# A long convolution over even tokens, odd tokens and their sums, in a hybrid decoder block on one core

## The chip, the cores and the metric

The kernel runs on one core of a Trainium2 chip. Its time is the device time of one execution in microseconds (us). Three executions of the kernel before were timed, and their median is the number that the change is held against; one further execution was profiled. The engines are TensorE (PE, matrix products; PEld is its loading of weights), VectorE (DVE), ScalarE (ACT), GpSimd (POOL) and SyncE (SP). In this kernel POOL does little but issue the transfers that add into their target, and SP issues the plain loads and stores.

## The reference, cut to what matters

One layer on 512 tokens of 1024 channels in fp32: a mixer of three branches, then a gated feed-forward part. The change is in branch B, a gated convolution of 31 taps along the tokens, each channel by itself, with a layer norm and a product behind it.

```python
h = rmsnorm(x, norm_mix_g); proj = h @ w_in     # splits into p_a, p_b, q, p_g
...
u, ug = jnp.split(p_b, 2, axis=-1)
u = u * jax.nn.sigmoid(ug)
u = _causal_dwconv(u, conv_b_w) + conv_b_bias   # y_t = sum_k w[k] u_{t-30+k}
u = jax.nn.silu(_layernorm(u, ln_b_g, ln_b_b))
y_b = u @ w_b_out
...
merged = g[:, :, 0] * y_a + g[:, :, 1] * y_b + g[:, :, 2] * y_c   # g: sigmoid gates
x = x + merged @ w_o
...
x = x + (jax.nn.silu(gt) * up) @ w_down         # gt, up: conv3(rmsnorm(x) @ w_up)
out = rmsnorm(x, norm_final_g)
```

## The kernel before

**Products.** Every large product is cut into two by two blocks and done with seven block products instead of eight (forms 1 to 7 of a "quad", `quad_loads`, `multiply`). Each operand is split into a high part (ScalarE rounds it, job `wh` for weights, L1220) and a low part (VectorE subtracts, job `wl`, L1224), and three products hi x hi, hi x lo, lo x hi are added up in PSUM. Some sums of weight blocks are made by a transfer that adds into its target, issued by POOL (`more`, L1374; `wadd` for w_o); others by VectorE.

**Layout and order.** Channels lie on the 128 partitions and tokens along a row; a tile holds two channel groups of 512 tokens. The channels of branch B make four pieces p = 0 to 3. There is no loop that sets the order: every step is a job with a key, an engine and its needs (`Jobs.add`), and the long list `PLAN` gives the order in which jobs are put into the program, the buffer that each new tile takes (sb0 to sb16, lf0 to lf5, wf0 to wf5, the PSUM banks ps0 to ps7), and sometimes one more job that it is held behind. `issue_in_program_order` makes each engine and each queue follow that order strictly, so an instruction that waits holds all behind it on its engine.

**Branch B.** For piece p, ScalarE makes the sigmoid (`sg`), VectorE multiplies (`um`) to give the tile u. The convolution then fills the tile acc:

- `("tap", p, 0)`, ScalarE, L2112: acc = u times the last weight, plus the bias, for each of the two channel groups.
- Taps s = 4, 8, .. 28, VectorE, L2129: one fused multiply-add into acc[s:] from u[:512-s] for each channel group.
- The other 23 taps of each piece (`ACT_TAPS`): ScalarE scales u into a tile of its own (`("tp", p, s)`, L2137), and VectorE adds the tile to acc (`("tap", p, s)`, L2149), one instruction for both groups.
- For the 18 taps in `PAIRED` (five in each of the first three pieces, three in the last) the products of taps s and s + 1 are joined first by a transfer that POOL issues (`("tj", p, s+1)`, L2143: it adds the second tile into the first), and VectorE adds both at once.

When all four pieces are done their sum over channels is made (`tot1`, `tot2`, `mu`), TensorE turns it into the mean (`("mu", "mean")`), and centring, squares, variance, `lns` and `swish` follow. The result is the input of the quads `("out", 1, i)`, with the first 256 tokens (`lo_t`) and the last 256 (`hi_t`) as the two token blocks.

**Merge.** `out_reads` weighs the blocks of `("out", 1, i)` with the gates: `by2` and `by3` treat the first and the second block of tokens of the gate tile m = 2i, `by4` and `by7` the same of m = 2i + 1. `("sum", 1, m, r)` (L2419) adds token half r of gate tile m to what the other branches gave. `mgh` and `mgl` split the merged rows into high and low parts (L2522, L2527); the steps `("ms", p)` make block differences (L2505, L1177); and the products with w_o follow in the order a, b, f, c, d, e, g, each in parts i = 0 and 1 (L1171 to L1173). Products a and b use token half 0. Before the change `("sum", 1, m, 0)` needs only `by2` (or `by4`) and `("sum", 1, m, 1)` only `by3` (or `by7`). The sum of weight blocks `("wsum", i)` (L1640) that c uses is made by VectorE.

**End.** The last products are `("pd", "g", "rest", i)` for the left and right 256 columns (i = 0, 1) of half of the last rows. ScalarE squares and sums each (`("sr", 3, i)`, L3086), `ends` adds the first sum into the second's companion (L3101), a root (L3104), a reciprocal, the scaling and the stores follow.

Of the kernel before, what the change touches and what calls it, by code (L numbers as in the profile page):

```python
# [8 lines left out]
F32 = mybir.dt.float32  # L9
# [5 lines left out]
P = 128  # L15
D = 1024
KC = D // P
SEQ = 512
# [48 lines left out]
ACT_TAPS = [s for s in range(1, 31) if s % 4]  # L67
PAIRED = [(p, s) for p in range(4) for s in (1, 5, 9, 17, 25) if p < 3 or s not in (5, 25)]
# [13 lines left out]
    (("mem tile", 0), "sb2"), (("ldm", 0, 0), ""), (("raw tile", "K"), "wf3"),  # L82
# [883 lines left out]
]  # L966


# [2280 lines left out]
```

## Time and profile before

| | |
|---|---|
| median of three executions | 888.43 us (888.05, 888.43, 890.31) |
| the profiled execution, its own time | 888.78 us |
| its span, first to last instruction | 886.8 us |
| granted TensorE clock | 0.999 |
| PE busy | 878.7 us, 6937 products |
| DVE busy | 827.2 us, 949 instructions |
| ACT busy | 701.4 us, 983 instructions |
| POOL busy | 168.3 us, 193 instructions |
| moved by DMA | 211.38 MB, mean 238 GB/s |

A row of a group reads: line, engine, operation, output <- inputs, shapes, count | busy us, mean ns of one | idle time of the engine just before, and what ended it. A row of the timeline reads: start us, us, engine, line, operation, names, shapes, count, then in brackets the idle time before it and who ended it. A row of the waits reads: who waited <- for whom: us in total, times, longest. A row of the stages reads: the stretch, its length, then busy us (and instructions) of PE, PEld, DVE, ACT and POOL, the granted clock, the share of the DMA engines and GB/s. The chain that ended last follows the work back from the last instruction and gives each engine's share of the span.

### The profile page before, as it was taken

Reading aid. Unit: us, or ns where it says so; the run is one execution under the profiler, and the core shown is the slowest. Engines: PE = TensorE matmul, PEld = TensorE weight load, DVE = VectorE, ACT = ScalarE, POOL = GpSimd, SP = SyncE. Lnnn points to the kernel's source line nnn. Section 1 sums busy time; section 2 is a strip of 40 time slices with the busy share of each in tenths; the row PEclk is TensorE's granted clock in tenths of the full one; section 3 lists DMA queues with packets and bytes.
Section 4 is the critical chain, followed back from the end, with each engine's and each line's share of the span. In section 5 each row is a group of like instructions: output and inputs, shape, how many; then the busy total and the mean of one; then the engine's idle time right before and its main releaser. Section 6 shows DMA issues by size and latency. Waiting matters only on the chain.

```text
span 886.8 us, 17492 instructions
## 1 busy us (share of the span) xinstructions
PE 878.7 (99%) x6937; PEld 848.8 (96%) x6937; DVE 827.2 (93%) x949; ACT 701.4 (79%) x983; POOL 168.3 (19%) x193
## 2 busy tenths in 40 slices
PE   9999999999999999999999999999999999999997
PEld 8999999999999999999899998899999999998886
DVE  6997889989999999999899999998899799999997
ACT  7587889979998788798889973877776677866665
POOL 0012222111222131221221211121121111101120
PEclk9999999999999999999999999999999999999999
DMA  9989999779999999998999999999999799689984
GB/s 352 340 194 234 228 254 233 143 148 211 248 232 265 235 266 218 240 245 223 245 228 257 238 251 283 300 261 244 240 236 260 177 262 190 160 284 331 268 180 131
DMA packets 62288, 211.38 MB, mean 238 GB/s; under 512 B 6784, under 2 KB 11776, under 8 KB 62208
## 3 DMA queue, kind: packets, MB, share of 16 engines
q0 software_dynamic: 28944, 96.00, 59.1%
q1 hardware_dynamic: 32976, 114.02, 35.6%
q8 instruction: 54, 0.88, 0.4%
q10 hardware_dynamic: 288, 0.27, 0.1%
q14 instruction: 26, 0.21, 0.1%
HBM read 194.23 MB, written 4.19 MB: 224 GB/s over the span
## 4 chain that ended last, share of the span: by engine, by line
PE 85%; DVE 6%; DMA 3%; ACT 3%; issue 2%; SPq 0%; POOL 0%; DVEq 0%; ACTq 0%
PE bank L1424 61%; PE bank L1173 6%; PE bank L1171 6%; PE bank L1172 6%; PE bank L1810 2%; DVE wlo L1224 2%; PE bank L2331 1%; PE bank L2333 1%; PE bank L2332 1%; DMA wf<-in_w_in 1%; DMA tp<-tp 1%; ACT whi L1220 1%; DVE fl L1338 1%; DMA wf<-in_w_v 1%; ACT tp L2137 1%
## 5 line engine op out<-in xcount | busy, mean ns | idle before, releaser
L1224 DVE TENSOR_TENSOR wlo<-wf,whi 128x1024 fp32r<-128x1024 f32 (+1 forms) x189 | 226.0, 1209 | 13.5 <-ACT whi L1220 13.1
L1220 ACT CAST whi<-wf 128x1024 fp32r<-128x1024 f32 x192 | 198.1, 1042 | 42.6 <-PE bank L1424 13.0
L2137 ACT ACTIVATE tp<-u,pk 128x495 f32<-128x495 f32 (+22 forms) x184 | 119.2, 712 | 4.7 <-DVE acc L2149 1.9
L2149 DVE TENSOR_TENSOR acc<-acc,tp 128x966 f32<-128x966 f32 (+17 forms) x74 | 87.7, 1185 | 4.0 <-DMA tp<-tp 2.1
L1374 POOL DMA_DIRECT2D wf<-in_w_in x48 | 45.9, 990 | 137.1 <-DVE wlo L1224 63.3
L1424 PE MATMUL bank<-fb10h,whi 128*128 128x256 f32 x232 | 64.1, 276 | 0.3 <-ACT bank L1458 0.3
L1424 PE MATMUL bank<-ft4h,whi 128*128 128x256 f32 x232 | 64.0, 276 | 0.0
L1424 PE MATMUL bank<-fb11h,wlo 128*128 128x256 f32 x232 | 63.9, 275 | 0.0
L1424 PE MATMUL bank<-ft7h,whi 128*128 128x256 f32 x232 | 63.9, 275 | 0.0
L1424 PE MATMUL bank<-fb11h,whi 128*128 128x256 f32 x232 | 63.9, 275 | 0.0
L1424 PE MATMUL bank<-fb00h,whi 128*128 128x256 f32 x232 | 63.9, 275 | 0.0
L1424 PE MATMUL bank<-fb00l,whi 128*128 128x256 f32 x232 | 63.8, 275 | 0.0
L1424 PE MATMUL bank<-fb00h,wlo 128*128 128x256 f32 x232 | 63.8, 275 | 0.0
L1424 PE MATMUL bank<-fb10l,whi 128*128 128x256 f32 x232 | 63.8, 275 | 0.0
L1424 PE MATMUL bank<-fb10h,wlo 128*128 128x256 f32 x232 | 63.8, 275 | 0.0
L1424 PE MATMUL bank<-ft5l,whi 128*128 128x256 f32 x232 | 63.8, 275 | 0.0
L1424 PE MATMUL bank<-ft5h,wlo 128*128 128x256 f32 x232 | 63.8, 275 | 0.0
L1424 PE MATMUL bank<-ft6l,whi 128*128 128x256 f32 x232 | 63.8, 275 | 0.0
L1424 PE MATMUL bank<-ft6h,wlo 128*128 128x256 f32 x232 | 63.8, 275 | 0.0
L1424 PE MATMUL bank<-ft7l,whi 128*128 128x256 f32 x232 | 63.8, 275 | 0.0
L1424 PE MATMUL bank<-ft7h,wlo 128*128 128x256 f32 x232 | 63.8, 275 | 0.0
L1424 PE MATMUL bank<-ft4l,whi 128*128 128x256 f32 x232 | 63.8, 275 | 0.0
(434 smaller groups left out, 3371.3 us busy)
## 6 DMA issues: line engine op xcount, KB each, us to landing
wf<-in_w_in POOLq DMA_DIRECT2D x48, 512.0 KB, 7.9
wf<-in_w_in SPq DMA_DIRECT2D x45, 512.0 KB, 6.4
wf<-in_w_up SPq DMA_DIRECT2D x29, 512.0 KB, 6.2
wf<-in_w_up POOLq DMA_DIRECT2D x26, 512.0 KB, 8.2
wf<-in_w_down SPq DMA_DIRECT2D x15, 512.0 KB, 5.3
wf<-in_w_a_out SPq DMA_DIRECT2D x8, 512.0 KB, 5.6
wf<-in_w_v SPq DMA_DIRECT2D x7, 512.0 KB, 6.1
wf<-in_w_kv SPq DMA_DIRECT2D x7, 512.0 KB, 6.8
```

The costliest lines, as they stand in the source:

```text
L1171: nc.tensor.matmul(ps, s_hi, w_hi, start=start, stop=False, skip_group_check=again)
L1172: nc.tensor.matmul(ps, s_hi, w_lo, start=False, stop=False, skip_group_check=again)
L1173: nc.tensor.matmul(ps, s_lo, w_hi, start=False, stop=stop, skip_group_check=again)
L1220: nc.scalar.copy(parts[0], src())
L1224: nc.vector.tensor_tensor(lo, src(), hi.bitcast(F32), op=ALU.subtract)
L1338: nc.vector.tensor_tensor(t, x, y.bitcast(F32), op=ALU.subtract)
L1374: nc.gpsimd.dma_start(out=tiles[key], in_=block(w, col[c], k), accum_op=ALU.add)
L1424: nc.tensor.matmul(ps[:, c, :], w[:, i, at], in_turns(a[i]), start=first and n == 0, stop=i == 3 and n == 2, skip_group_check=again,)
L1810: nc.tensor.matmul(ps[:, j, :], w[:, k, at], in_turns(a[:, k, :]), start=first and j == 0 and k == 0 and n == 0, stop=g == 1 and k == 3 an ...
L2137: nc.scalar.activation(two(("tp", p, s))[:, j, s:], two(("u", p))[:, j, : SEQ - s], AF.Copy, scale=weight(j),)
L2149: nc.vector.tensor_tensor(a, a, two(("tp", p, at))[:, :, at:], op=ALU.add)
L2331: nc.tensor.matmul(ps, w_hi[:, i, at], hi, start=first, stop=False)
```

## The change

Split the tokens of u into even ones e and odd ones o, and the 31 weights, counted by their delay s, into even delays a (16) and odd delays b (15). The even outputs are a\*e plus b\*o delayed by one; the odd outputs are (a+b)\*(e+o) - a\*e - b\*o. So three filters of 16, 15 and 16 taps over 256 tokens are run per channel group. The tile acc holds a\*e in its first half (r = 0) and b\*o in its second (r = 1); the new tile `cs` holds (a+b)\*(e+o) and e+o. For each k from 1 to 15:

- `("tp", p, k)`, ScalarE: for both groups and both r, u's tokens r, r + 2, .. times the weight of delay 2k + r, 256 - k elements each (k = 15 has r = 0 alone), into one tile;
- `("tap", p, k)`, VectorE: adds that tile to acc; for the ten (p, k) in the new `PAIRED` (k = 1, 7, 13 for three pieces, k = 1 for the last) the tiles of k and k + 1 are joined first by a transfer;
- `("tc", p, k)`, VectorE: two multiply-adds from e+o into the third filter.

New beside them: `("cse", p)` (e+o, VectorE), a start on ScalarE of six instructions (256 elements each), `ole`, `ev` and `od` on VectorE, which put the three filters together, and once `w_sum` (a+b) and `bias_2`. The finished acc holds the even tokens first and then the odd ones, and stays so through the layer norm and the quads of branch B; `out_reads` therefore applies the gates to tokens 0, 2, 4 .. and 1, 3, 5 .., and a token half of the merged sum needs both blocks. `("wsum", 0)` becomes a transfer on POOL. `PLAN` is written anew: the same steps of TensorE, with neighbours swapped in places, other buffers and other holds.

```diff
-ACT_TAPS = [s for s in range(1, 31) if s % 4]
-PAIRED = [(p, s) for p in range(4) for s in (1, 5, 9, 17, 25) if p < 3 or s not in (5, 25)]
+PAIRED = [(p, k) for p in range(4) for k in (1, 7, 13) if p < 3 or k == 1]
...
 def out_reads(q, gates, sigmoids):
+        first, second = (slice(0, SEQ, 2), slice(1, SEQ, 2)) if q[1] == 1 else (lo_t, hi_t)
         def by_bank(i, b):
-            t = parted(gate[i]()[:, :, lo_t])
+            t = parted(gate[i]()[:, :, first])
         def by_tile(i):
-            t = gate[i]()[:, :, hi_t]
+            t = gate[i]()[:, :, second]
...
+        def u_of(j, r, n, p=p):
+            return two(("u", p))[:, j, :].rearrange("p (n r) -> p r n", r=2)[:, r, :n]
+        def u_summed(p=p, u_of=u_of, both_of=both_of):
+            make(("cs", p))
+            t = tiles["u", p].rearrange("p (j n r) -> p j r n", j=2, r=2)
+            nc.vector.tensor_tensor(both_of(1), t[:, :, 0, :], t[:, :, 1, :], op=ALU.add)
...
+            def tap_product(k=k, p=p, rs=rs, u_of=u_of, w=tap_weight):
+                make(("tp", p, k))
+                t = tiles["tp", p, k].rearrange("p (j r n) -> p j r n", j=2, r=2)
                 for j in range(2):
+                    for r in rs:
+                        nc.scalar.activation(
+                            t[:, j, r, k:], u_of(j, r, HALF - k), AF.Copy, scale=w(2 * k + r, j))
+            def tap_add(at, rs, p=p, acc_of=acc_of):
+                t = tiles["tp", p, at].rearrange("p (j r n) -> p j r n", j=2, r=2)
+                a = acc_of()[:, :, rs.start : rs.stop, at:]
+                nc.vector.tensor_tensor(a, a, t[:, :, rs.start : rs.stop, at:], op=ALU.add)
+            def sum_tap(k=k, both_of=both_of, ws=sum_weight):
+                for j in range(2):
+                    a = both_of(0)[:, j, k:]
+                    nc.vector.scalar_tensor_tensor(
+                        a, both_of(1)[:, j, : HALF - k], ws(k, j), a, op0=ALU.mult, op1=ALU.add)
+        def odd_less_even(both_of=both_of, acc_of=acc_of):
+            nc.vector.tensor_tensor(
+                both_of(0), both_of(0), acc_of()[:, :, 0, :], op=ALU.subtract)
+        def even_done(acc_of=acc_of):
+            a = acc_of()[:, :, 0, 1:]
+            nc.vector.tensor_tensor(a, a, acc_of()[:, :, 1, : HALF - 1], op=ALU.add)
+        def odd_done(both_of=both_of, acc_of=acc_of):
+            a = acc_of()[:, :, 1, :]
+            nc.vector.tensor_tensor(a, both_of(0), a, op=ALU.subtract)
...
-                    by = weighed[r : r + 1] if br in OUT_QUADS else weighed
+                    by = weighed
...
-            [("wadd", "x", i), ("wl", ("wo", "d", i))], use=[("wo", "x", i), ("wo", "y", i)]))
+            [("wadd", "x", i), ("wl", ("wo", "d", i))], use=[("wo", "x", i), ("wo", "y", i)])
+            if i else job(
+            ("wsum", i), "POOL", MORE, lambda: nc.gpsimd.dma_start(
+                out=tiles["wo", "y", i], in_=tiles["wo", "x", i], accum_op=ALU.add),
+            [("wadd", "x", i), ("wl", ("wo", "d", i))], MORE_LATENCY,
+            use=[("wo", "x", i), ("wo", "y", i)]))
```

From the new list, the steps of TensorE, VectorE and ScalarE (and `wsum`) from the end of branch B to w_o's b, and the order of the two last products:

```
(("out",1,0),3)  by7(1) by4(0) wl(out,1,1,3) r3(0)  (("out",1,1),3)  by3(0) sum(1,0,1) sum(1,0,0)
sum(1,1,1)  (("out",1,1),4)  mgh(a,0) r3(1) mgl(a,0) by3(1) sum(1,1,0)  (wo,a,0)  by4(1) mgh(a,1)
mgl(a,1) sum(1,2,1) sum(1,2,0)  (wo,a,1)  wsum(0) sum(1,3,1) mgh(b,0) sum(1,3,0) wh(d,1) ms(f)
wn(d,1) mgl(b,0) mgh(f) ms(c)  (wo,b,0)  mgh(b,1) wl(f,0) wh(f,1) wh(c,0) mgl(b,1) mgl(f)  (wo,b,1)
...
(pd,g,5)  (pd,g,rest,0)  ...  (pd,g,rest,1)          before: rest 1, then rest 0
```

More of the change, by code (lines that the diff above doesn't have):

```diff
@@ L614 @@
-    (("sum", 1, 1, 0), ""), ((("out", 1, 1), 3), ""), (("r3", ("out", 1, 0)), ""),
-    (("mgh", "a", 1), ""), (("wl", ("wo", "a", 1)), ""), (("mgh", "b", 0), "sb3"),
-    (("wl", ("wo", "d", 0)), "", (("out", 1, 0), 3)), (("by3", ("out", 1, 0)), ""),
-    ((("out", 1, 1), 4), ""), (("mgl", "a", 1), ""), (("r3", ("out", 1, 1)), ""),
-    (("sum", 1, 0, 1), "sb12"), (("wadd", "x", 0), "", (("out", 1, 1), 3)),
[105 rows of a table removed]
-    ((("cf", 1, 1), "done"), ""), ((("cf", 1, 0), "done"), ""), (("silu", 1), ""),
[18 rows of a table removed]
-    ((("cf", 2, 1), "done"), ""), ((("cf", 2, 0), "done"), ""), (("silu", 2), ""),
[34 rows of a table removed]
@@ new lines @@
+    (("r2", ("gate", 1, 1)), "sb10"), (("var", "sum"), ""), ((("gate", 1, 1), 6), ""),
+    (("wh", ("merge", 0, 3, 1)), ""), (("r3", ("gate", 1, 0)), ""),
+    (("sum", 0, 2), "", ("r2", ("gate", 1, 1))), (("var", "fold"), ""), (("sigmoid", 1, 0), ""),
[5 rows of a table added]
+    (("table", "swish"), ""), (("wl", (("gate", 1, 1), 4)), ""),
+    (("ld", (("out", 1, 0), "u")), "lf2", ("v", "squares")), (("wh", ("wo", "b", 1)), ""),
+    (("v", "rows"), "ps5"), (("ld", (("out", 1, 1), "s")), "wf2", ("v", "squares")),
+    (("r5", ("gate", 1, 1)), "sb14"), ((("gate", 1, 1), 7), ""), (("lns", 0), ""),
[3 rows of a table added]
@@ new lines @@
+    (("wadd", "x", 1), "", (("out", 1, 0), 4)), (("by3", ("out", 1, 0)), ""),
+    (("sum", 1, 0, 1), "sb13"), (("ld", ("wo", "y", 1)), "lf4", ("r6", ("out", 1, 1))),
+    (("sum", 1, 0, 0), "sb2"), (("sum", 1, 1, 1), ""), ((("out", 1, 1), 4), ""),
[5 rows of a table added]
+    (("wsum", 0), "", ("mgl", "a", 1)), (("sum", 1, 3, 1), ""), (("mgh", "b", 0), "sb8"),
[98 rows of a table added]
+    ((("cf", 1, 0), "done"), ""), ((("cf", 1, 1), "done"), ""), (("silu", 1), ""),
[122 rows of a table added]
+    ((("cf", 8, 0), "done"), ""), ((("cf", 8, 1), "done"), ""), (("silu", 8), ""),
[115 rows of a table added]
@@ L1124, in scaled_act @@
         return n / 1160.0 + 0.175 + extra
-    TAP = 0.665
+    TAP, TAP_HALF = 0.665, 0.4
     MM, MM_HALF, MM_QUAD = 0.2158, 0.114, 0.1119
@@ L2112, in conv_start @@
                 nc.scalar.activation(
-                    two(("acc", p))[:, j, :], two(("u", p))[:, j, :], AF.Identity,
-                    bias=par("conv_b_bias", 2 * p + j),
-                    scale=par("conv_b_w", (K_B - 1) * KC + 2 * p + j),
-                )
-        job(("tap", p, 0), "ACT", 2 * scaled_act(512, 0.09), conv_start,
-            [("um", p), ("ldp",)] + ([("tap", p - 1, K_B - 4)] if p else []),
-            take=[(("acc", p), ANY)], use=[("u", p)])
-        made_taps = []
@@ L2172, in first_sum @@
+        both_use = [("acc", p), ("cs", p)]
+        job(("ole", p), "DVE", dve(512), odd_less_even, [made_taps[-1], ("tc", p, K_B // 2)],
+            use=both_use)
+        job(("ev", p), "DVE", dve(512), even_done, [("ole", p)], use=[("acc", p)])
+        job(("od", p), "DVE", dve(512), odd_done, [("ev", p)], use=both_use)
+    conv_done = [("od", p) for p in range(4)]
     def first_sum(key, a, b):
```

297 lines of the change are left out of this document (143 added, 154 removed), and 1534 rows, old and new, of the table PLAN.

## The prediction

> **What bounds the kernel now.** I read the profile's page first (engine sums, the chain that ended last), then the stages, then who made TensorE wait, and only then the groups the change touches.
>
> ```profile
> span 886.8 us, 17492 instructions
> ...
> PE 878.7 (99%) x6937; PEld 848.8 (96%) x6937; DVE 827.2 (93%) x949; ACT 701.4 (79%) x983; POOL 168.3 (19%) x193
> ...
> PE 85%; DVE 6%; DMA 3%; ACT 3%; issue 2%; SPq 0%; POOL 0%; DVEq 0%; ACTq 0%
> ```
>
> TensorE (PE) is busy 99% of the span and carries 85% of the chain that ended last. VectorE (DVE) at 93% looks nearly as full, but carries 6%. The kernel is bound by TensorE; the question is how much of its 886.8 - 878.7 = 8.1 us of idle time the change can reach.
>
> ```profile
> 1.05 3.78 PE L2734 MATMUL bank<-ones 128*128 128x128 f32 x16 [1.05 <-DVE ones L2737]
> ```
> ```profile
> 881.04 0.28 PE L1173 MATMUL bank<-whi,zl 128*128 128x256 f32 x1
> 881.35 0.38 ACT L3086 ACTIVATE j<-bank 128x256 f32<-128x256 f32 x1 [1.20 <-PE bank L1173]
> 881.63 0.19 ACT L3086 ACTIVATION_READ_ACCUMULATOR j<-bank 128x1 f32 x1
> 881.86 0.16 DVE L3101 SCALAR_TENSOR_TENSOR cols<-cols 128x1 f32<-128x1 f32 x1 [1.67 <-ACT j L3086]
> 882.05 0.29 ACT L3104 ACTIVATE cols<-cols 128x1 f32<-128x1 f32 x1 [0.23 <-DVE cols L3101]
> ```
>
> 1.05 us lie before the first product and 886.8 - 881.32 = 5.5 us behind the last one. So only 8.1 - 1.05 - 5.5 = 1.6 us of idle time stand inside the run. The waits of TensorE name them:
>
> ```profile
> PE bank L2734 <- DVE ones L2737: 1.1, 1, 1.1
> PE bank L1171 <- ACT ob L2032: 0.7, 1, 0.7
> PE bank L1424 <- ACT bank L1458: 0.3, 1, 0.3
> PE bank L1173 <- DVE ql L1944: 0.2, 1, 0.2
> PE bank L1810 <- DVE wlo L1224: 0.2, 1, 0.2
> PE bank L1173 <- DVE mgl L2527: 0.2, 1, 0.2
> ```
>
> The first row is the start; the other five sum to 1.6 us. The stages say the same of the stretch where the long convolution runs:
>
> ```profile
> 200.00:300.00 100.00, 100.00 (x876) 99.36 (x875) 96.66 (x109) 92.08 (x135) 24.48 (x26) 1.00 1.01 237
> 300.00:400.00 100.00, 99.74 (x890) 99.39 (x890) 98.47 (x105) 85.20 (x121) 22.44 (x25) 1.00 1.02 242
> 400.00:500.00 100.00, 100.00 (x716) 94.59 (x716) 93.16 (x101) 88.89 (x122) 18.98 (x21) 1.00 0.98 238
> ```
>
> After the window and its length come PE, its weight loads, DVE, ACT and POOL busy in us. TensorE is idle 0.26 us in 300. VectorE and ScalarE (ACT) run close to full beside it and keep up.
>
> **The change part by part.** *The products.* The new order holds the same 386 groups of TensorE steps, some swapped with a neighbour; no product goes. TensorE: 0.
>
> *The convolution's arithmetic.* Taps 4, 8 .. 28 were multiply-adds on VectorE, the others were scaled by ScalarE and added by VectorE, some after a joining transfer.
>
> ```profile
> L2137 ACT ACTIVATE tp<-u,pk 128x495 f32<-128x495 f32 (+22 forms) x184 | 119.2, 712 | 4.7 <-DVE acc L2149 1.9 <-DVE yal L2259 1.1 <-DMA tp<-tp 0.7
> L2149 DVE TENSOR_TENSOR acc<-acc,tp 128x966 f32<-128x966 f32 (+17 forms) x74 | 87.7, 1185 | 4.0 <-DMA tp<-tp 2.1 <-ACT tp L2137 0.5
> L2129 DVE SCALAR_TENSOR_TENSOR acc<-u,pk,acc 128x508 f32<-128x508 f32 (+6 forms) x56 | 38.5, 728 | 0.1
> L1882 DVE SCALAR_TENSOR_TENSOR hb<-x,pk,rows 128x256 f32<-128x256 f32 x16 | 6.4, 473 | 0.0
> L2112 ACT ACTIVATE acc<-u,pk 128x512 f32<-128x512 f32 x8 | 6.1, 806 | 0.4 <-DVE u L2105 0.4
> L1525 DVE TENSOR_TENSOR g<-g,yy 128x512 f32<-128x512 f32 x8 | 5.5, 684 | 0.0
> ```
> ```profile
> 7.54 0.91 ACT L1591 ACTIVATE mh<-mem,pk 128x256 fp32r<-128x256 f32 x2
> ```
> ```profile
> 540.93 1.21 DVE L1640 TENSOR_TENSOR wo<-wo,wo 128x1024 f32<-128x1024 f32 x1
> ```
>
> VectorE loses 87.7 + 38.5 us, and 1.2 us for the weight sum that becomes a transfer: 127.4. It gains the summed filter, 15 steps x 2 halves x 4 pieces = 120 multiply-adds of under 256 elements, at 6.4/16 = 0.40 us in a row of such: 48.0 (at 473 ns each, were none to overlap, 56.8); 60 - 10 = 50 adds, 46 of about 1000 elements at 1.185 = 54.5 and four of half that at 0.68 = 2.7; 16 steps of 512 (the sum of even and odd tokens, and three to close each piece) at 0.68 = 10.9. Two more steps run once, on the weights and the biases, at most 0.68 each by the same row. Sum 116.1 without them, so VectorE is relieved of some 10 to 11 us (1 to 2.5 at the dear end). ScalarE loses 119.2 + 6.1 = 125.3 and gains 232 scalings and 24 starts of under 256 elements, at 0.91/2 = 0.455: 116.5, so 9 us less. That bound is soft: the trace shows no ScalarE read of every second element in SBUF. If each short step cost what a long one does now (119.2/184 = 0.648), it would be 166, 41 us more. I take 0.455, because reads of every second element are in this trace from PSUM (line 1470 reads its bank so), and they cost nothing:
>
> ```profile
> L1470 DVE TENSOR_TENSOR gt<-gt,bank 128x512 f32<-128x512 f32 x14 | 9.5, 681 | 0.2 <-PE bank L1424 0.2
> ```
>
> 681 ns against 684 ns for line 1525, which reads SBUF in order. [...]
>
> In time all this is worth 0: both engines lie beside TensorE, which is idle 0.26 us in the stretch where the saving falls. The cover that hides the saving is TensorE's own queue.
>
> *The joins.* Eighteen joining transfers become ten. One wait of the present order comes from a join:
>
> ```profile
> 186.26 2.01 ACT L1940 ACTIVATE qh<-qq 128x1024 fp32r<-128x1024 f32 x2 [3.14 <-DMA tp<-tp]
> ```
> ```profile
> 186.26 2.48 DVE L2149 TENSOR_TENSOR acc<-acc,tp 128x1022 f32<-128x1022 f32 x2 [2.11 <-DMA tp<-tp]
> ```
>
> Both engines stand until a join lands, the query parts come late, and TensorE pays twice soon after: 0.7 for ob and 0.2 for ql. In the new order the summed filter's steps, which need no transfer, stand ahead of that add, and the score products are elsewhere. I take -0.9; between 0 (another step late in their place) and -0.9.
>
> *The merge behind branch B.* This is where the change adds a wait. The tokens of branch B now come out as even and odd, so each half row of the merged sum needs two products of gate and branch (by2 and by3, or by4 and by7) where it needed one. The first half rows, which the w_o products a and b use first, now wait for the last products of branch B.
>
> ```profile
> 534.26 0.38 PE L1171 MATMUL bank<-whoh,mgh 128*128 128x512 f32 x1
> ```
> ```profile
> 579.41 2.68 PE bank L1424 x24
> ```
> ```profile
> 868.22 0.38 PE L1172 MATMUL bank<-wlo,zh 128*128 128x512 f32 x1
> 868.43 0.38 PE L1173 MATMUL bank<-whi,zl 128*128 128x512 f32 x1
> ```
> ```profile
> 535.05 0.74 DVE L1518 SCALAR_TENSOR_TENSOR g<-bank,g 128x256 f32<-128x256 f32 x2
> 535.72 0.68 DVE L2419 TENSOR_TENSOR mg<-g,g 128x512 f32<-128x512 f32 x1
> 536.32 0.68 DVE L2527 TENSOR_TENSOR mgl<-mg,mgh 128x512 fp32r<-128x512 f32 x1
> 536.92 1.22 DVE L2505 TENSOR_TENSOR mg<-mg,mg 128x1024 f32<-128x1024 f32 x1
> 538.05 1.22 DVE L1224 TENSOR_TENSOR wlo<-wo,whi 128x1024 fp32r<-128x1024 f32 x1
> ```
>
> Starts tell the pace on VectorE: 0.60 us for 512 elements, 1.13 for 1024, 0.67 for the pair. TensorE takes 2.68 us for 24 products of 256 columns, and 12 x 0.215 = 2.6 for each part of a and b. Let 0 be the start of the product (out,1,1),3; the (out,1,0),3 before it is then done. Nine steps of 512 stand in the new order (r3, by3, three sums, r3, the low part of a's first half, by3, a sum): 0.2 + 5.4 = 5.6, with a's first part needed at 5.4 and ready at 4.5. Then by4 0.67, a's second low part 0.60: 6.9, needed at 8.0. Then four sums 2.4, the difference f 1.13, b's first low part 0.68: 11.1, needed at 10.55, so TensorE stands 0.6. Then the difference c, a weight's low part and b's second low part reach 14.0 against 13.7, another 0.25. Together 0.85 against 0.2 in the same place now (the wait for mgl): +0.6. I bound it by -0.2 (no wait at all) and +2 (VectorE 1.4 us late at time 0, somewhat more than one 1024-element step).
>
> *The weight sum by transfer* is queued on POOL behind a's second low part (at 6.9), ahead of two other weight adds there, and ScalarE has the high part of w_o's c queued behind its landing.
>
> ```profile
> tp<-tp POOLq DMA_DIRECT2D x4, 510.0 KB, 7.1
> ```
>
> It lands near 6.9 + 7.1 = 14, plus 1 for the queue; c begins behind a, b and the four parts of f, near 5.4 + 10.4 + 0.85 + 5.2 = 21.8. High and low part take 2.2 us, so 4 us of cover remain: 0. Landing 4 us later it would be paid one for one.
>
> *The end.* The two last products change places, so the square that comes last writes where the root reads, and the add at 881.86 is done before: the root follows the square directly, 882.05 - 881.82, about -0.2.
>
> **Sum.** The profiled execution took 888.78 (886.8 span and 2.0 around it): 888.78 - 0.9 + 0.6 - 0.2 = 888.3. That execution lies 0.35 above the median of the three runs, 888.43; against the median I predict 887.9.
>
> **Rivals.** *Faster:* every wait inside goes, 1.6, and the end gives 0.2: 886.6. To pass 0.3% (2.7 us, about what a measurement of this kernel tells from none) another 0.9 must come from the start or from products stretched by a late operand that no wait row lists: 885.5. For it: 11 us of relief on VectorE. Against: the windows from 200 and from 400, in which TensorE is never idle, have nothing to give. *Slower, by reads of every second element:* ScalarE 41 us dearer over the stretch of the adds:
>
> ```profile
> L2149 DVE TENSOR_TENSOR acc<-acc,tp x74: 1153/1184/1224, 95.3 to 457.1; 128x1022 f32<-128x1022 f32 x4, 128x1018 f32<-128x1018 f32 x4, 128x1014 f32<-128x1014 f32 x4, 128x1010 f32<-128x1010 f32 x4
> ```
>
> That is 362 us, so 11 in each 100: 92 + 11 = 103 in the window from 200, 3.1 us too many, the next two at 96 and 100, an estimated 1 us more: 892. It decides from about 0.6 us a step. Against it stands the PSUM row. *Slower, by the merge:* VectorE comes late to time 0 above. It has 5.6 us of work for 5.4 of TensorE's there, so what it is late goes on to TensorE one for one, and from 3.2 us of lateness the run is slower by over 0.3%: 891.2 at 3.3. Against it: in the profile of before by4 started at 535.05, only some 0.5 us behind the end of its product (534.26 + 0.28). *The change brings nothing it says:* a second order of the same work has new small waits for the old ones, 888.4; it lies within my forecast.
>
> **How the numbers follow.** My forecast, within 0.3% (885.8 to 891.1), 0.73: nothing on TensorE's path is taken away, and the terms sum to -0.5. Faster 0.14. Slower 0.13: reads 0.05, merge or another stage whose wait grows like it 0.08. The terms' own ends give 888.43 - 0.9 - 0.2 - 0.2 = 887.1 and 888.43 + 2 = 890.4; to hold 8 in 10 the range reaches into both rivals, 885.5 to 891.0.
>
> **What would show it.** In the new profile: PE busy again 878 to 879 us with 6937 products; DVE near 817 and ACT near 692; the 256-element scalings near 0.4 to 0.46 us in a row; ten tp joins and no TensorE wait for ob or ql; a wait for mgl of about 0.6 near 540. I am wrong if TensorE's idle time inside the run passes 4 us or the scalings take 0.6 us.

## The result and the profile after

| | before | after |
|---|---|---|
| median of all runs beside each other | 889.18 us (888.05 to 890.31, 4 runs) | 897.90 us (895.24 to 899.30, 4 runs) |
| profiled execution, its span | 888.78, 886.8 | 897.00, 895.2 |

The changed kernel is slower: the ratio is 1.0099, 95% interval 1.0081 to 1.0118. The forecast was 887.9 (885.5 to 891.0). One execution of one later kernel, e13, ran at a granted clock of 0.753 and is left out; e16 is the same kernel again.

The page of the changed kernel, its first lines and the chain:

```profile
span 895.2 us, 17542 instructions
...
PE 882.3 (99%) x6937; PEld 849.8 (95%) x6937; DVE 820.8 (92%) x1006; ACT 705.1 (79%) x1047; POOL 159.7 (18%) x186
...
PE 30%; DVE 0%; ACT 0%; issue 0%; DVEq 0%
```

VectorE fell by 6.4 us, ScalarE rose by 3.7, TensorE still has 6937 products, and the span grew by 8.4. (The chain is followed for only 30% of the span here, so it can't be set beside the 85% of before.) The waits of TensorE name places (columns: sum in us, times, longest):

```profile
PE bank L2244 <- ACT mu L2218: 1.3, 1, 1.3
PE bank L1151 <- DVE x L2626: 1.1, 1, 1.1
PE bank L2778 <- DVE ones L2781: 1.1, 1, 1.1
PE bank L1404 <- ACT bank L1438: 0.8, 2, 0.6
PE bank L1404 <- DVE wlo L1204: 0.8, 1, 0.8
PE bank L2244 <- DVE mu L2222: 0.6, 1, 0.6
PE bank L1153 <- DVE mgl L2571: 0.5, 1, 0.5
PE bank L1152 <- DVE wlo L1204: 0.5, 1, 0.5
```

The waits for ob and ql of before are gone; new ones stand at the channel mean (mu, L2244), in w_o (L1151 to L1153) and at weight tiles (wlo). Waits leave out products that were only stretched (TensorE is busy 882.3 us for its 6937 products here, 878.7 before), so I use a second reading throughout: **lateness**, the start of the n-th TensorE product in a kernel minus the start of the n-th in the profile of before. Both kernels have the same 6937 products.

| n-th product, its time before | 3200th, 380 us | 3750th, 456 | 3900th, 474 | 4400th, 536 | 4450th, 547 | 4800th, 598 | 5400th, 665 | last, 881 |
|---|---|---|---|---|---|---|---|---|
| after: late by | -1.42 | -0.11 | 2.91 | 2.71 | 3.34 | 5.82 | 8.24 | 8.57 |

So 1.4 us are gained by 380 us; then 4.3 are lost between 380 and 474 us (1.3 before the mean, with one TensorE wait of 0.60 us at 415 us, and 3.0 at the mean), 0.6 at the merge, 2.5 in w_o behind it, 2.4 at the start of the up projection. Behind the last product 0.2 is gained.

The first loss is a loss of VectorE's time. Stretches of 15 us before and behind the last adds, first in the kernel before, then in the changed one (after the window: PE, PEld, DVE, ACT, POOL busy in us):

```profile
440.00:455.00 15.00, 15.00 (x83) 13.46 (x82) 14.47 (x17) 15.00 (x24) 4.07 (x5) 1.00 1.01 204
455.00:470.00 15.00, 15.00 (x123) 14.60 (x122) 14.87 (x16) 11.00 (x15) 2.62 (x3) 1.00 1.04 248
```
```profile
440.00:455.00 15.00, 15.00 (x83) 13.47 (x82) 11.55 (x16) 13.52 (x24) 3.63 (x5) 1.00 0.97 200
455.00:470.00 15.00, 12.78 (x97) 11.72 (x96) 14.88 (x19) 10.83 (x15) 1.76 (x2) 1.00 0.93 196
```

Before, VectorE is idle 0.66 us of the 30; after, 3.57. The difference, 2.9, is as large as the lateness behind the mean; the runs below show what causes it. VectorE stands idle first, while TensorE is still fully busy, and TensorE pays 10 us later. What VectorE waits for, in the changed kernel (ScalarE's and VectorE's timelines, then TensorE's):

```profile
448.27 2.17 ACT L2152 ACTIVATE tp<-u,pk 128x243 f32<-128x243 f32 x4
451.68 2.16 ACT L2152 ACTIVATE tp<-u,pk 128x242 f32<-128x242 f32 x4 [1.24 <-DVE acc L2164]
```
```profile
453.87 1.17 DVE L2164 TENSOR_TENSOR acc<-acc,tp 128x968 f32<-128x968 f32 x1 [1.02 <-ACT tp L2152]
454.95 1.22 DVE L1204 TENSOR_TENSOR wlo<-wf,whi 128x1024 fp32r<-128x1024 f32 x1
456.19 0.66 DVE L2164 TENSOR_TENSOR acc<-acc,tp 128x482 f32<-128x482 f32 x1
456.88 0.69 DVE L2191 TENSOR_TENSOR cs<-cs,acc 128x512 f32<-128x512 f32 x1
```
```profile
464.33 0.51 PE L2244 MATMUL bank<-mu,mean_w 128*128 128x512 f32 x1 [1.35 <-ACT mu L2218]
```

ScalarE makes the products of one delay step in four short instructions, 2.17 us. It then waits 1.24 us for VectorE's add, because the next products go to the same buffer, and VectorE then waits 1.02 us for ScalarE. The two work in turn instead of side by side. Behind the last add (456.19) stand three closing steps, the sum, the fold and the mean's parts.

### The profile page after: what moved, and what is told of

Its sections match the earlier page's. It is cut to its first block, busy times and chain, and to the rows that moved or that the text cites. A ratio compares the mean times of both kernels' runs of the same rounds, so it can differ in the third digit from the quotient of the medians.

```text
span 895.2 us, 17542 instructions
## 1 busy us (share of the span) xinstructions
PE 882.3 (99%) x6937; PEld 849.8 (95%) x6937; DVE 820.8 (92%) x1006; ACT 705.1 (79%) x1047; POOL 159.7 (18%) x186
## 5 line engine op out<-in xcount | busy, mean ns | idle before, releaser
L1204 DVE TENSOR_TENSOR wlo<-wf,whi 128x1024 fp32r<-128x1024 f32 x204 | 244.3, 1212 | 22.7 <-ACT whi L1200 19.5
L1200 ACT CAST whi<-wf 128x1024 fp32r<-128x1024 f32 (+1 forms) x207 | 213.9, 1046 | 38.8 <-PE bank L1404 11.4
L2152 ACT ACTIVATE tp<-u,pk 128x255 f32<-128x255 f32 (+14 forms) x232 | 114.8, 585 | 3.6 <-DVE acc L2164 2.4
L1354 POOL DMA_DIRECT2D wf<-in_w_in x57 | 50.9, 951 | 209.8 <-PE bank L1404 48.4
L1404 PE MATMUL bank<-ft6h,whi 128*128 128x256 f32 x232 | 64.0, 276 | 0.2 <-ACT gt L1434 0.2
L1404 PE MATMUL bank<-ft5h,whi 128*128 128x256 f32 x232 | 63.9, 275 | 0.0
L1404 PE MATMUL bank<-ft4h,wlo 128*128 128x256 f32 x232 | 63.8, 275 | 0.0
```

The source lines that it names most:

```text
L1200: nc.scalar.copy(parts[0], src())
L1204: nc.vector.tensor_tensor(lo, src(), hi.bitcast(F32), op=ALU.subtract)
L1354: nc.gpsimd.dma_start(out=tiles[key], in_=block(w, col[c], k), accum_op=ALU.add)
L1404: nc.tensor.matmul(ps[:, c, :], w[:, i, at], in_turns(a[i]), start=first and n == 0, stop=i == 3 and n == 2, skip_group_check=again,)
L2152: nc.scalar.activation(t[:, j, r, k:], u_of(j, r, HALF - k), AF.Copy, scale=w(2 * k + r, j))
```

## The experiments

All are compared with the kernel before on the same chip. "Lost" is the growth of lateness in the profiled execution. The first four were written for four theories: A, ScalarE's short steps hold back the last piece's adds; B, VectorE's own queue behind the last add (three closing steps and two weight tiles' low parts) makes the mean late; C, the new list's order is worse whatever the steps cost; D, the weight sum's transfer lands late and holds ScalarE, VectorE and TensorE in turn.

| run | median us | ratio to before, 95% | lost 380 to 474 | at 474 late by | lost 547 to 598 | lost 598 to 665 |
|---|---|---|---|---|---|---|
| after | 897.90 | 1.0081 to 1.0118 | 4.3 | 2.9 | 2.5 | 2.4 |
| e10 (kernel before) | 891.98 | 1.0018 to 1.0044 | 2.0 | 2.3 | 1.3 | 0.0 |
| e17 | 893.18 | 1.0031 to 1.0069 | 0.2 | -1.9 | 2.1 | 2.7 |
| e16 | 897.13 | 1.0068 to 1.0106 | 0.7 | 1.5 | -0.3 | 2.4 |
| e13 (as e16, three executions) | 896.15 | 1.0054 to 1.0098 | | | | |
| e18 | 893.69 | 1.0035 to 1.0073 | 0.4 | 0.2 | -0.3 | 2.3 |
| e1 | 895.58 | 1.0052 to 1.0095 | 4.0 | 2.1 | 2.3 | 3.6 |
| e9 | 895.48 | 1.0047 to 1.0090 | 4.2 | 3.3 | 1.9 | 2.3 |
| e3 | 897.63 | 1.0080 to 1.0133 | 5.9 | 4.3 | -0.3 | 2.3 |
| e6 | 898.15 | 1.0085 to 1.0115 | 4.6 | 3.1 | 1.5 | 2.5 |
| e11 | 897.53 | 1.0059 to 1.0116 | 6.0 | 5.6 | 2.3 | 2.8 |
| e14 | 897.96 | 1.0079 to 1.0121 | 4.9 | 3.4 | 2.3 | 2.0 |
| e2 | 896.08 | 1.0058 to 1.0107 | 4.2 | 3.6 | 1.1 | 2.3 |
| e5 | 896.31 | 1.0061 to 1.0107 | 2.4 | 2.0 | 0.8 | 3.8 |
| e7 | 904.66 | 1.0143 to 1.0195 | 6.6 | 6.3 | -0.3 | 0.3 |
| e4 | 896.15 | 1.0048 to 1.0105 | 3.7 | 2.2 | 1.1 | 1.0 |
| e8 | 893.51 | 1.0035 to 1.0065 | 2.9 | 2.6 | 1.1 | 0.0 |
| e12 | 894.85 | 1.0033 to 1.0073 | 4.8 | 4.6 | 0.1 | 0.2 |
| e15 | 895.53 | 1.0045 to 1.0086 | 4.6 | 4.6 | -0.2 | 1.3 |

One warning for this table: after, e2, e4 and e5 are the same program up to 474 us, and stand there at 2.9, 3.6, 2.2 and 2.0 us. e7 is the same program up to the mean, and its first product of the mean comes 3.8 us late, against 1.4, 2.1, 0.7 and 0.5 in those four. Even at 380 us the profiles of the new list stand between 2.0 us early and 0.8 late, and the 1.3 us lost before the mean in the changed kernel are not lost in e5. Single executions differ by that much, so at the mean only e17 and e18, whose medians fell too, say something by themselves.

**Has VectorE time to spare?** e10, on the kernel before:

```
+        for _ in range(3 if key == ("tot",) else 1):
             nc.vector.tensor_tensor(tiles[key], tiles[a], tiles[b], op=ALU.add)
...
+            for _ in range(2 if p == "d" else 1):            # low part of the merged d
+            for _ in range(2 if unit in ((("up", 5), 1), (("up", 5), 2)) else 1):   # wl
```

> On the kernel before, with its own order: VectorE repeats work that it has done anyway, in three places: the first sum of the mean twice more (2.3 us, near 451), the low part of the merged d once more (1.1 us, near 550), and the low parts of two weight tiles of the up projection once more each (2.3 us in all, near 690). If VectorE has no time to spare in the first two stages and TensorE follows it, the lateness grows by about 1.8 to 2.3 us at the mean and by about 1.1 us in the w_o stage, by nothing at 690, and the time is 892 to 892.6. If VectorE's idle 8 per cent cover such things, as the forecast had it, the time stays at 889.2.

VectorE's added work at the mean and the first TensorE wait behind it:

```profile
450.47 3.74 DVE L2176 TENSOR_TENSOR tot<-acc,acc 128x1024 f32<-128x1024 f32 x3
```
```profile
PE bank L2207 <- ACT mu L2181: 0.6, 1, 0.6
```

Lost: 2.0 us at the mean for 2.3 added, 1.3 in w_o for 1.1 added, 0.4 near 670 (where the third addition fell) for 2.3 added. The median is 891.98, 3.2 above the kernel before beside it (888.77). In the first two stages VectorE's added time is nearly all paid by TensorE, although VectorE is busy only 93% of the span; in the third it nearly isn't.

**Why is the mean late?** Three runs that move nothing in the order. e17, ScalarE's time of the last piece:

```
+                if p == 3:
+                    nc.scalar.activation(t[:, :, :n_r, k:], u[:, :, :n_r, : HALF - k],
+                                         AF.Copy, scale=w(2 * k, 0))
+                    return
```

> The changed kernel with one longer step of ScalarE (about 1.1 us) in place of the four (2.1 us) for each delay of the last piece alone; all of that piece's even and odd products and both its channel blocks take one weight, so its result isn't the reference's. VectorE's work is unchanged. If ScalarE's time is what starves VectorE before the mean, the lateness gained there falls from 2.9 to 1 us or less. If VectorE's closing steps or the buffers that the products wait for set it, it stays at 1.5 to 3.

e16 (and e13 before it), VectorE's closing steps of the last piece:

```
         def odd_less_even(both_of=both_of, acc_of=acc_of, p=p):
+            if p == 3:
+                return
...          (the same in odd_done)
```

> On the changed kernel with its own order: two of the three closing steps of the last piece are left out (the subtraction of the even result from the sums and the last subtraction, 0.69 and 0.68 us of VectorE, so that piece's odd results are not what the reference has). If every microsecond of VectorE in front of the mean is paid by TensorE, the lateness gained at the mean falls from 2.9 to 1.5 us and the time by about 1.4, to about 896.5. If the transfer's landing or ScalarE sets the mean, it stays near 2.9.

> The edit of e13 once more, since its profiled execution ran at a granted clock of 0.753 and can't be read by stages: two closing steps of the last piece left out, 1.37 us of VectorE. If VectorE's work in front of the mean is paid one for one, the lateness gained at the mean falls from 2.9 to about 1.5 us; if ScalarE or a landing sets it, it stays near 2.9.

e18 is both edits:

> Both edits of the two runs beside it: one step of ScalarE for each delay of the last piece, and its two closing steps left out. If the two causes add, the mean is no longer late: the lateness gained there is between minus 0.3 and 0.4 us, and the time is 2.5 to 3 us below the changed kernel's, about 895. If something else sets the mean, 1 us or more remains.

e17's loss is gone altogether. Its last adds and the mean, VectorE's timeline of e17:

```profile
449.21 1.17 DVE L2169 TENSOR_TENSOR acc<-acc,tp 128x968 f32<-128x968 f32 x1 [0.45 <-ACT tp L2152]
450.30 1.22 DVE L1204 TENSOR_TENSOR wlo<-wf,whi 128x1024 fp32r<-128x1024 f32 x1
451.43 0.65 DVE L2169 TENSOR_TENSOR acc<-acc,tp 128x482 f32<-128x482 f32 x1
```

The last add starts at 451.43 instead of 456.19, and the mean's first product at 460.92 instead of 464.33, where the same program without the edit spread from 463.4 to 466.7. TensorE does not wait for the mean, and the median falls by 4.7 us (the ratio from 1.0099 to 1.0050). One step of about 1.5 us (1.41 to 1.61) in place of four that take 2.1 was enough: ScalarE's time per delay in the last piece sets the mean. e16 stands at 1.5 us late where the changed kernel stood at 2.9: by 1.4, the 1.37 us that were taken away. But its first product of the mean came only 0.6 earlier (463.75), which is inside the spread, so this one execution does not show that VectorE's closing steps count. Its median did not fall; in the profile the next stage lost 5.1 us, most of it to a transfer (below). e18 has no wait for the mean either, but since e17 alone removes it, e18 can't show whether the two edits add.

e1 shortens ScalarE's time less:

```
-                    for r in rs:
-                        nc.scalar.activation(
-                            t[:, j, r, k:], u_of(j, r, HALF - k), AF.Copy, scale=w(2 * k + r, j))
+                    nc.scalar.activation(
+                        t[:, j, :n_r, k:], u[:, :n_r, : HALF - k], AF.Copy, scale=w(2 * k, j))
```

> The changed kernel, but ScalarE scales even and odd tokens of a tap in one step with the even tap's weight (116 longer steps in place of 232 short ones; the odd delays thus get the wrong weights). It takes away ScalarE's cost per short step and nothing from VectorE or the order. Theory A (short steps on ScalarE hold the last piece's adds back, so the channel mean comes late): the adds wait for no scaling any more, the mean's product starts about 3 us earlier (464.3 to about 461.5), and the run gains 2.5 to 3 us. Theory B (VectorE's own queue behind the last add makes the mean late: three closing steps and two weight lows before it): the last add comes earlier by the waits seen, 1 to 2 us, and the mean by as much at most. Theory C (the order of the whole list is worse, whatever the steps cost): no gain over 0.5 us.

The median fell by 2.3, a little less than A wanted; the mean's product started at 463.49, not near 461.5, and the place at 474 (2.1 instead of 2.9) lies inside the warning. Its steps were dearer than planned, 0.85 us each instead of 0.65 (last section), so it took little of ScalarE's time away, and e17 is the better test.

The rest of these runs try to mend the order in front of the mean by moving entries of the list or giving a tile another buffer. e9 (the job is also allowed to take a `wf` buffer):

```
-    (('tp', 3, 13), 'sb3'),
+    (('tp', 3, 13), 'wf1'),
```

> One edit on the changed kernel: the products of delay step 13 of the last piece go to a buffer of the weights' ring, so ScalarE no longer waits for VectorE's add of step 13 before it writes step 14 (1.24 us of wait in the changed kernel; both steps shared one buffer). If VectorE's idle time in front of the last adds is what the mean pays, the mean product starts about 1.2 us earlier, the lateness gained there falls from 2.9 to about 1.8 us, and the time to about 896.7. If VectorE's queue behind the last add is the limit, neither moves.

The wait of 1.24 us was gone and the mean's share of the loss fell from 3.0 to 2.1 us, as expected in size; the median fell by 2.4, but the stretch as a whole lost as much as before. By the warning above this stays undecided. e3 and e6 shorten VectorE's queue behind the last add (`wl` of form 4 behind `("mu", "low")`; in e6 also `tot2` right behind `tot1`):

> The changed kernel, with one entry moved: VectorE's low part of the weight of (gate,1,0),4 goes from before the closing step od of the last piece to behind the low part of the mean's sums. Theory B: the mean comes 1.1 us earlier (one 1024-element step) and the run gains about 1.1 us. Theory A: 0 to 0.3 us, since ScalarE's lateness is ahead of it.

> Two edits on the changed kernel: the weight low part for form 4 of gate (1,0) moves behind the mean's low part on VectorE (as before), and the transfer that adds the third pair's result into the sum moves to right behind the first add in GpSimd's order, ahead of a weight add that was held. If it was this transfer's landing (461.4 us) that kept the mean late once VectorE's queue was shortened, the mean product starts at 462.8 to 463.4 instead of 464.3 and the time falls by 1.0 to 1.5, to about 896.5. If the last adds themselves are late (short ScalarE steps), the mean stays within 0.4 us of where it was, and so does the time.

Neither helped. In e3 the sum then waited 0.90 us for the transfer `tot2`. In e6 it did not, and the mean's product started at 463.39, as was expected for the transfer; but the same program as the changed kernel reached 463.4 too (e5). In both runs form 4 waited 1.4 us for VectorE right behind the mean: here the work that was put off was missed a little later. e11 (e9, and `("sigmoid", 0, 2)` and one weight tile's two parts behind the last products) and e14 (e9, and the tile for which ScalarE waits at 420 us behind step 7):

> On the changed kernel, three local edits in front of the mean: the second buffer as in the run beside it; one sigmoid (two steps, 1.3 us) moved behind the last full products; and one weight tile's high and low part moved behind the last products and the last add. ScalarE then reaches the last products about 2.5 to 3.7 us earlier. If ScalarE's steps and waits starve VectorE there, the lateness gained at the mean falls from 2.9 to between 0 and 1 us and the time to about 895.3. If not, it stays at 1.8 or more and the time at 896.7.

> Two local edits on the changed kernel: the second buffer for step 13, and one weight tile's high part and scaled part (for the merge of branch A) moved behind the products of step 7 on ScalarE. In the changed kernel ScalarE waited 3.9 us for that tile's load at 420 to 424 us with step 7 queued behind it, and VectorE stood idle 2.4 us. If such waits of ScalarE are where VectorE's time before the mean went, step 7 starts 4 to 5 us earlier, and the lateness gained between 400 and 470 us falls from 4.2 to 1 to 2 us; the time is 894 to 895.5. If VectorE's work alone sets it, it stays at 3.3 or more, as with the second buffer alone.

Both failed. In e11 VectorE waited 1.18 us for the last products, since the tile that used to fill that time was now behind them. In e14 step 7 waited 3.57 us for its buffer in place of the load, and the tile that I had moved came 2.9 us late for its own product. None of the moves that were tried brought the mean back.

**w_o.** The path of the weight sum in the changed kernel, over POOL, ScalarE, VectorE and TensorE:

```profile
539.36 0.86 POOL L2525 DMA_DIRECT2D wo<-wo  x1 [1.98 <-DVE mgl L2571]
```
```profile
549.72 1.06 ACT L1200 CAST whi<-wo 128x1024 fp32r<-128x1024 f32 x1 [4.43 <-DMA wo<-wo]
550.68 1.03 ACT L2566 CAST mgh<-mg 128x1024 fp32r<-128x1024 f32 x1
```
```profile
551.75 1.23 DVE L2571 TENSOR_TENSOR mgl<-mg,mgh 128x1024 fp32r<-128x1024 f32 x1 [2.26 <-ACT mgh L2566]
```
```profile
554.86 0.45 PE L1151 MATMUL bank<-whi,mgh 128*128 128x512 f32 x1 [1.11 <-DVE x L2626]
```

The transfer lands 10.3 us behind its issue. ScalarE holds the merged high part c behind it, VectorE stands idle 2.26 us, and TensorE's lateness grows by 2.5 us up to 559 us, with waits of 1.11 us (554.86) and 0.49 (558.77). e2 moves `("wh", ("wo", "c", 0))` behind `("mgh", "d")`; e5 gives the sum back to VectorE, behind `("ms", "c")`:

> The changed kernel, with one entry of the list moved: ScalarE's high part of w_o's c, which waits for the weight sum by transfer, goes behind the high parts of the merged rows c and d instead of ahead of them. Theory D (the transfer lands late and holds what is queued behind it on ScalarE, from there VectorE's low part and row adds, from there TensorE): the waits at 553 to 559 us, 2.5 us in sum, go or fall to 0.5, and the run gains about 2 us. Rival (the wait is in the merge's new dependency, not in the transfer): they stay.

> One edit on the changed kernel: the weight sum for c of half 0 is done by VectorE again (1.2 us, behind the merged difference c) instead of by a transfer from GpSimd's queue. If the transfer's landing is what is late (10.3 us from issue to the end of ScalarE's wait in the changed kernel), the waits of TensorE at 553 to 559 us go, the lateness gained in the w_o stage falls from 3.1 to about 1 us, and the time to about 895.5. If instead VectorE's own queue is the limit there, the sum's 1.2 us pushes the row adds and c's low part back by as much, and the time stays at 897 to 899.

In e2 the loss fell from 2.5 to 1.1. In e5 it fell to 0.8, but the part before it (536 to 547 us) rose from 0.6 to 1.8, where b's low part now came behind the sum: together 2.6 against 3.1. So VectorE's 1.2 us cost about as much as the transfer did. e12 (below) issues the transfer without the hold and puts c's high part behind the function table's load (1.28 us), and loses 0.1, though the landing took 12.2 us there. With e2 that points to the transfer's place, and not to the transfer itself.

A second transfer comes in from e16, its tile whol (low part of b's weights):

```profile
L1221 POOL DMA_DIRECT2D whol<-in_w_o x3: 859/859/862, 527.5 to 543.4; - x3
...
  PE bank L1152: 3.6, 1
...
DMA to landing us min/median/max: 8.4/8.5/8.9
```

POOL issues b's at 535.99 here and at 536.52 in the changed kernel; before, at 524.00. In the changed kernel it lands 5.4 us later, and the product that uses it starts at 542.37: 0.4 us to spare. In e16 it lands 8.9 us later, and TensorE waits 3.6. What moved it is the new list's place for the load of these weights, which SP issues at 492.32 before, at 525.61 in the changed kernel and at 524.51 in e16; ScalarE rounds and scales the tile behind that, and in e16 it waits for the load itself:

```profile
533.17 1.05 ACT L1200 CAST whoh<-wf 128x1024 fp32r<-128x1024 f32 x1 [0.90 <-DMA wf<-in_w_o]
```

In the changed kernel the scaling also stands behind a's high part, which waits 1.82 us for the merged sum. So the change took this transfer's cover away. The same wait, 2.5 to 3.3 us, is in the profiles of e3, e4 and e18. How much of the spread among executions comes from it was not measured.

**The order of the list.** e4 takes before's order of all jobs from behind w_o's c; e7 takes before's order, merge and weight sum from the mean on:

> The changed kernel up to the last step of w_o's c, and from there the order of the list of before (its buffers too, where they are free). No arithmetic differs from the changed kernel. Theory C for the third stretch of lost time (2.4 us at 607 to 624 us, in the up projection, which the convolution's change does not touch): the waits there go, and the run gains about 2.4 us. Rival (the lateness is handed down from the stages before): they stay, whatever the order.

> The changed kernel up to the channel mean, then the kernel before: its order of all work from the mean on, its merged sums over the two contiguous halves of the tokens (so branch B's tokens are added in another order than the output wants), each of which needs only its own half of the branch, and the weight sum on VectorE. If merge, transfer and order behind the mean are what costs the later 5.5 us, the lateness stays flat from 470 us on (within 0.7) and the time is 891.5 to 892.5. If the later losses are only what the late mean leads to, they stay and the time is 896 to 898.

In e4 the stretch from 598 to 665 us lost 1.0 us instead of 2.4, and the median fell by 1.8. In that stretch every profile with the new list loses 2.0 to 3.8 us, those with the old order 0.0 to 1.3 (e4, e7, e8, e12, e15). There the new list has the loads for the first weight tiles of the up projection in another order. In the changed kernel ScalarE waits for one, and behind it TensorE:

```profile
606.46 1.05 ACT L1200 CAST whi<-wf 128x1024 fp32r<-128x1024 f32 x1 [2.21 <-DMA wf<-in_w_up]
```
```profile
608.82 0.38 PE L1404 MATMUL bank<-fb11h,wlo 128*128 128x256 f32 x1 [0.77 <-DVE wlo L1204]
```

Which load's place is at fault was not tried by itself. e7 otherwise failed as an experiment: it was already 3.8 us late at the mean's first product, where it is still the changed kernel's program, and TensorE later waited 4.2 us for one merged low part alone. I take it that the old order expects VectorE's work to be further on there than it was; that was not tried by itself.

**All together.** e8 is the w_o edit of e2, e6 and e4's order; e12 and e15 have e4's order and the earlier transfer, with e11's and e14's mean stage:

> Four local edits together, with the computation of the changed kernel: form 4's weight low part behind the mean, the sum's transfer earlier, the high part of w_o c behind the merged high part d, and the list of before from behind w_o c. If the parts' gains add (1.0 to 1.5 at the mean, 1.3 in w_o, 1.4 in the up projection), the time is about 894; if they stand in for one another, 895.5 to 896.5. In neither case does it beat the kernel before (889.3).

> All repairs together, with the computation of the changed kernel: the mean stage of the run beside it; in w_o the weight sum's transfer without its hold on a merged low part, and c's high part behind the function table's load, where ScalarE stands idle; and the list of before from behind w_o c. If the parts add (1.4 us gained before the mean, 0.5 lost there, 0.6 at the merge, 0.3 in w_o, none behind it, 0.2 gained at the end), the time is 889 to 890.5, the same as before. If an unlisted cost of the changed convolution remains, it stays above 892.

> The repairs of the run beside it, the sum's transfer earlier, the w_o edits (the weight sum's transfer without its hold, c's high part behind the table load) and the list of before from behind w_o c, all with the computation of the changed kernel. If they add: 1.4 us gained before 380 us, 1 to 2 lost before the mean, 0.6 at the merge, 0.2 behind it: 888.5 to 890.5, the same as before. If the changed convolution costs more than these places show, 892 or more.

e8 came out at 893.51, as the sum of its parts had it; e12 (894.85) and e15 (895.53) missed the 889 to 890.5 that they were to reach. None beats the kernel before; e8 is best at 1.0050 (1.0035 to 1.0065). In all three the losses behind the mean are down to 2 us or less, and 2.6 to 4.6 us at 474 remain.

## Why the prediction was wrong, point by point

- **The arithmetic, "in time all this is worth 0: both engines lie beside TensorE".** This is the step that failed. Where it put 0, the profiled execution lost 4.3 us up to and at the mean (2.4 to 4.2 in e2, e4 and e5), and e17, which only shortens ScalarE's time in the last piece, loses 0.2 there and takes 4.7 us off the median. I took TensorE's full windows from 200 and from 400 as proof of cover. They show that VectorE arrived in time, not by how much. e10 measures the margin: 2.3 us more work cost 2.0. And the convolution's end has a date, the mean, which is in none of my terms.
- **ScalarE's short steps.** Taken at 0.455 us from one row of two instructions near the start, measured 114.8/232 = 0.495 over all and 2.17/4 = 0.54 in the last piece:

```profile
L2152 ACT ACTIVATE tp<-u,pk 128x255 f32<-128x255 f32 (+14 forms) x232 | 114.8, 585 | 3.6 <-DVE acc L2164 2.4
L2164 DVE TENSOR_TENSOR acc<-acc,tp 128x1020 f32<-128x1020 f32 (+13 forms) x50 | 57.3, 1146 | 6.4 <-ACT tp L2152 6.1
L2169 DVE SCALAR_TENSOR_TENSOR cs<-cs,w_sum 128x255 f32<-128x255 f32 (+13 forms) x112 | 47.6, 471 | 0.0
```

  The middle row has 6.4 us of VectorE's idle time in front of its adds, 6.1 of it for ScalarE's products; this is the wait that e17 shows to be behind the loss. VectorE's adds were priced right (57.3 against 57.2). Its summed filter took 47.6/112 = 0.425 us a step instead of 0.40. ScalarE's total came out 3.7 higher instead of 9 lower. The rival "reads of every second element" was closer than its 0.05 in one half of its mechanism: ScalarE too slow for the adds is what e17 shows. The other half, that such reads are dear, is not shown (L2130 and L2132 in the last section, 0.59 us each), and its price of 0.6 us was too high against the 0.495 measured.
- **The joins, -0.9.** Right in number, but in part by luck. The waits for ob and ql are gone, and at 198 us every profile of the new list is 1.0 to 1.9 us early (-1.25 in the changed kernel). But e10, which is the kernel before up to 451 us, is 1.02 us early there as well: its ScalarE waits for the join 2.06 us where the profile of before had 3.14, and neither ob nor ql is late. Soon behind, another join holds it, and at 240 us it is 1.1 late:

```profile
204.11 1.22 DVE L2150 TENSOR_TENSOR acc<-acc,tp 128x1014 f32<-128x1014 f32 x1 [2.37 <-DMA tp<-tp]
```
```profile
205.98 0.66 PE L2066 MATMUL bank<-ident,pr 128*128 128x128 f32 x4 [1.19 <-DVE ptl L1998]
```

  So the term priced one execution's wait. That fewer joins spare TensorE some such wait fits both profiles of the old list; how much they spare over many executions was not measured.
- **The merge, +0.6.** Right in its own place: 0.63 between 536 and 547 us. What is in none of my terms is the transfer for b's weights, whose load stands later in the new list: 0.4 us to spare here, 3.6 of wait in e16.
- **The weight sum, "4 us of cover remain: 0".** The landing took 10.3 us, not 8.1 (7.1 of the joins and 1 for the queue, my estimate, which no row gave), and behind it stood not two parts but five steps in a row (c's weights high, c merged high and low, weights low, a row add), 549.72 to 554.71, 5.0 us instead of 2.2. Together 5.0 us later than reckoned, against a cover of 4: 1.0, and TensorE's first wait is 1.11.
- **The products, "TensorE: 0", and the rival "a second order of the same work has new small waits".** The new order's waits in the up projection are 2.4 us, not small.
- **The end, -0.2.** Right: 0.18.
- I had named TensorE's idle time inside the run above 4 us as the sign of being wrong. It came: 895.2 - 882.3 - 1.1 at the start - 5.3 at the end = 6.5.

## What to carry to other kernels

A full TensorE says that the other engines are in time, not that they have time: before pricing work on VectorE or ScalarE at nothing, find the dates at which TensorE takes what they make (a mean, a merge, a first weight tile), and read VectorE's idle time in the 20 to 30 us before each, not over the span. Where that idle time is near zero, as here (0.66 of 30 us), what is added or waited is nearly all paid (2.0 of 2.3 us in e10). For a step that will wait on a transfer, count everything that is queued behind it on its engine up to TensorE, and take the slow landings (8.9 to 12.2 us here), not a median (6.6 for the joins).

## What the runs showed of the hardware that I had not expected

- On ScalarE an instruction over two interleaved rows of every second element took longer (0.85 us in e1) than one over about as many neighbours (0.65 before). The rows of before (495 neighbours), of e1 (496 elements in two rows of 248) and of the changed kernel:

```profile
L2137 ACT ACTIVATE tp<-u,pk 128x495 f32<-128x495 f32 x8 | 5.2, 705 | 0.0
```
```profile
L2152 ACT ACTIVATE tp<-u,pk 128x496 f32<-128x496 f32 x8 | 6.8, 901 | 0.5 <-DVE acc L2164 0.5
```
```profile
L2152 ACT ACTIVATE tp<-u,pk 128x248 f32<-128x248 f32 x16 | 8.2, 595 | 0.6 <-DVE acc L2164 0.6
L2132 ACT ACTIVATE cs<-cs,bias,w_sum 128x256 f32<-128x256 f32 x8 | 4.7, 587 | 0.0
L2130 ACT ACTIVATE acc<-u,pk 128x256 f32<-128x256 f32 x8 | 4.7, 587 | 0.0
```

  6.8/8 = 0.85 against 5.2/8 = 0.65 us. Yet at 256 elements a read of every second one (L2130) took what a read in order took (L2132), 4.7/8 = 0.59 us. So the stride alone was not shown to cost; the 0.2 us come from the two rows in one instruction, or from something else that e1 does differently. One row of 248 elements, every second one, took 8.2/16 = 0.51 us in the changed kernel, one of 495 neighbours 0.65 in the kernel before: with half the elements the time fell by a fifth.
- A transfer that adds a 512 KB tile in SBUF into another took 10.3 us in w_o, in the changed kernel and in e16, and 12.2 in e12. Joins of about that size in the convolution took 6.6 (5.0 to 8.3) in the changed kernel, but up to 10.5 in the kernel before (4.9 to 10.5, median 7.0).
- Two executions of one program differ by 3.3 us at one place (the mean's first product, 0.5 us late in e5 and 3.8 in e7, which differ only behind it). e12's ten executions spread over 6.5 us (890.01 to 896.52), the 22 of the kernel before beside them over 4.6 (887.24 to 891.85). Why landings and these places vary so was not tried.
